# Keys and values as one level of Strassen products in a two-layer decoder trunk

## The chip, the cores and the metric

One core of a Trainium2 chip runs the whole program in one launch. The metric is the device time in microseconds of one execution; lower is better. The median of three timed runs of the kernel before is 1442.52 us (1442.39 to 1442.74).

## The reference

Two layers; `x` is 512 tokens by 1024 features, all in float32. Of each layer this matters here:

```
h = rmsnorm(x) * (1 + sc1(c)) + sh1(c)          # 1024 features
u = h @ w_in                                    # pool, conv, q, k, v (512 columns each of q, k, v), 3 x 1024 gate logits
k = rope(rmsnorm(k)); q = rope(rmsnorm(q))      # 8 heads of 64
y_attn = block-sparse attention(q, k, v)
merged = sig(gate1)*(y_pool @ p_pool) + sig(gate2)*(y_conv @ p_conv) + sig(gate3)*(y_attn @ p_attn)
x = x + g1(c) * (merged @ w_out)                # g1, sc1, sh1, ...: rows of c_act @ w_ada
x = x + g2(c) * SwiGLU(...)
```

## The kernel before, in words

**Products.** Every float32 product is made of three TensorE matmuls at a faster type: each operand is split into a high part (rounded by ScalarE) and a low part (the rest, by VectorE), and `mm3` adds high*high, high*low and low*high. Activations are kept as 8 tiles of 128 features by 512 tokens, `norm.hi[k]` and `norm.lo[k]` (called `big` in the rows). A weight chunk is 128x1024: it is fetched into `raw` by SyncE's DMA queue, its high part `whi` is an ACTIVATE (L328), its low part `wlo` a TENSOR_TENSOR (L331). Chunks of gate columns get their low part by a transfer that adds onto a negated high part instead (`split_by_transfer`, L339 to L343).

**Order on TensorE.** It is written out by hand and kept: q with the first pool and conv columns, four more column tiles, then keys and values, then pool and conv tiles with the attention's pieces between them, the 16 gate tiles of the first two branches, the third gate's 8 tiles (`GATE2`), the 8 `attn` tiles with their merges, the 8 `out` tiles, and the feed-forward part (which already uses Strassen-like sums, class `Sums`).

**Keys and values.** `wide()` makes the keys, then a second `wide()` the values: 4 chunks each, 24 matmuls 128x512 a chunk, into four PSUM banks (one for each 128 tokens). Key banks are copied and squared by ScalarE and their squares summed by VectorE (`qk_evac`, L608 to L611). After the keys `rstds` (L597 to L604) and `scale_k` and `rope` (L989, L626 to L629) run on VectorE beside the values.

**Side work.** `bulk` is a queue of VectorE tasks with costs. Each 2048 columns of matmul are a tick, at which tasks are issued as far as a credit allows that grows by `bulk_rate`; `flush_bulk` issues all of them. Before, the eight dots for `g1` (`gains`, L399: one 128x1024 SCALAR_TENSOR_TENSOR on 512 KB of `w_ada`) lie in it: four beside the keys, four beside the values. `fibers` hold the attention's pieces, which are issued by tick as well; `drain` issues what is left of them.

**End of the attention.** Each `attn` tile is 12 matmuls; its merge is a gating (L1033), an addition (L1067) and a split (high part L572 on ScalarE, low part L573 on VectorE) into `merged[j]`, which all 8 `out` tiles read.

VectorE, ScalarE and each DMA queue work strictly in the order in which the program gives them their instructions; the tables further down show that order.

Of the kernel before, what the change touches and what calls it, by code (L numbers as in the profile page):

```python
# [57 lines left out]
NCOL = 74  # L58

# [20 lines left out]
def hybrid_trunk(ctx, tc, xT, ws, ada, cols, pool_w, qk_w, crow, pos, con, out):  # L80
# [210 lines left out]

    def feed_forward():
# [186 lines left out]
    class Norm:  # L479
        def __init__(self, one=False):  # L480
            self.one = one
            self.low = []
            self.acc = bigt(F32)
            self.last = bigt(F32)
            self.sums = [(bigt(), bigt()) for _ in range(1 if one else 2)]
            self.rstd = bigt(F32)
            self.hi = [bigt() for _ in range(KT)]
            self.lo = [bigt() for _ in range(KT)]

# [43 lines left out]
        def apply(self, l, i, k, lo, hi):  # L533
# [14 lines left out]
            if i == 1:  # L548
                A.activation(self.h[k][:, lo:hi], t[:, lo:hi], AF.Identity, bias=sh)
# [11 lines left out]
        def first_lo(self, k):  # L561
            pin(V.scalar_tensor_tensor(self.lo[k], self.t, mod[0][:, SH1, k:k + 1], f32(self.hi[k]),  # L562
                                       op0=ALU.add, op1=ALU.subtract))

# [42 lines left out]
    def qk_evac(which, qk, ss, t, src):  # L607
        A.activation(qk[t][:, which], src.rearrange("p (h d) -> p h d", d=HD), AF.Copy)  # L608
        sq = tmp()
# [221 lines left out]
    for l in range(L):  # L831
# [47 lines left out]
        def wide():  # L879


            pr = ps_pair()
            groups = [ps_mm(), ps_mm(), pr[:, 0], pr[:, 1]]
            for c in range(4):
                w = next_w()
                order = [(kk, t) for kk in range(2) for t in range(TT)]
                for kk, t in sorted(order, key=lambda o: o[1]) if c == 3 else order:
                    k = 2 * c + kk
                    mm3(groups[t], cut(norm.k(k), slice(None), slice(t * P, (t + 1) * P)),
                        wrow(w, 4 * kk), k == 0, k == KT - 1)  # L890
            return groups
# [79 lines left out]
        gains = ada_tasks(l, (G1,))  # L971
        bulk.extend(gains[:4])
        k_ps = wide()
        for t in range(TT):
            qk_evac(1, qk, ss, t, k_ps[t])
        flush_bulk()
# [14 lines left out]
        bulk.append((1.6, rstds))  # L991
        for t in range(TT):
            bulk.append((1.5, lambda t=t: (scale_k(t), rope(qk, t, wc, wsn))))
        bulk.extend(gains[4:])


        v_ps = wide()
        v = [[bigt().rearrange("p (n h d) -> p n h d", n=4, h=2) for _ in range(TT)] for _ in range(2)]
        for t in range(TT):
            for half in range(2):  # L1000
                src = v_ps[t][:, half * BLOCK:(half + 1) * BLOCK].rearrange("p (n d) -> p n d", d=HD)
                o = v[half][t]
                A.activation(o[:, :, 0], src, AF.Copy)
                V.tensor_sub(o[:, :, 1], src, f32(o)[:, :, 0])
        flush_bulk()


        m01, y_attn = [], []
        fibers.append([3, attention(l, qk, v, nrq, prq, y_attn)])
# [13 lines left out]

        def gate():
            g = ps_mm()
            feature_tile(g, next_w())
            sg = bigt(F32)
            A.activation(sg, g, AF.Tanh, scale=0.5)  # L1028
            return sg
# [21 lines left out]
        sg2 = {}  # L1051
        merged = []
        aw_ = None
        for step, j in GATE2:
            if step == "gate":
                sg2[j] = gate()
                continue
            if j == 0:
                drain()
            if j % 2 == 0:  # L1060
# [74 lines left out]
        n2.h = [bigt(F32) for _ in range(KT)]  # L1135
# [251 lines left out]
```

## Time and profile before

| | before |
|---|---|
| median of runs | 1442.52 us |
| profiled execution, own time | 1442.24 us |
| its span in the trace | 1440.5 us |
| TensorE / VectorE / ScalarE busy | 1433.7 / 1014.5 / 714.0 us |
| instructions on TensorE / VectorE / ScalarE | 8346 / 1858 / 1199 |
| moved by DMA | 241.83 MB, mean 168 GB/s |

The execution's own time is 1.74 us longer than the span between the first and last instruction of the trace. All other times are read from that span's start. A row of the timeline gives start, duration, engine, line, operation, the tile written and the tiles read, and in brackets how long the engine had been idle and what released it.

### The profile page before, as it was taken

What the parts mean: (1) busy time and instruction counts of PE and PEld (TensorE: products, weight loads), DVE (VectorE), ACT (ScalarE), POOL (GpSimd) and SP (SyncE); (2) the same over time, 40 slices, a digit from 0 to 9 for tenths busy, and PEclk for the clock granted to TensorE, in tenths of its full rate; (3) what the DMA queues carried; (4) which work ended last, traced back from release to release, by engine and by line L of the source; (5) the groups of instructions that cost most, each with busy time, mean ns of one, the idle gap of its engine ahead of it and who ended that gap; (6) DMA issues with size and microseconds to landing.
All of it is one profiled execution on the core that took longest, in us unless ns stands there. A gap on an engine that the chain in (4) does not pass through costs nothing.

```text
span 1440.5 us, 21954 instructions
## 1 busy us (share of the span) xinstructions
PE 1433.7 (100%) x8346; PEld 1261.7 (88%) x8346; DVE 1014.5 (70%) x1858; ACT 714.0 (50%) x1199; POOL 145.7 (10%) x204
## 2 busy tenths in 40 slices
PE   9999999999999999999999999999999999999999
PEld 7888888888988998999988888888889989999997
DVE  8887777649686867677798766654578747657663
ACT  5645666733653452535444466666336625525450
POOL 0000110101100311210000000011020102111200
PEclk9999999999999999999999999999999999999999
DMA  9647876665347766756536565567372537637532
GB/s 351 216 149 209 220 184 168 181 229 163 90 140 223 187 179 206 190 146 198 189 125 207 177 146 135 135 154 194 129 208 85 136 114 180 173 105 187 136 88 85
DMA packets 91049, 241.83 MB, mean 168 GB/s; under 512 B 11576, under 2 KB 24256, under 8 KB 90944
## 3 DMA queue, kind: packets, MB, share of 16 engines
q1 hardware_dynamic: 67312, 177.37, 36.8%
q0 software_dynamic: 23040, 62.93, 22.3%
q8 instruction: 65, 1.06, 0.3%
q14 instruction: 40, 0.33, 0.1%
q10 hardware_dynamic: 592, 0.14, 0.0%
HBM read 238.30 MB, written 2.10 MB: 167 GB/s over the span
## 4 chain that ended last, share of the span: by engine, by line
PE 96%; issue 1%; DMA 1%; DVE 1%; ACT 0%; ACTq 0%; DVEq 0%; POOLq 0%
PE mm L151 83%; PE pair L151 12%; PE mm L157 1%; DMA wlo<-in_ws 1%; DMA colt<-in_cols 0%; DVE big L788 0%; DVE big L795 0%; DVE big L562 0%; ACT whi L339 0%; DVE w L399 0%; ACT big L1028 0%; DVE wlo L331 0%; ACT big L575 0%; DVE tmp L555 0%; ACT big L559 0%
## 5 line engine op out<-in xcount | busy, mean ns | idle before, releaser
L151 PE MATMUL mm<-big,whi 128*128 128x512 f32 (+1 forms) x4350 | 1078.0, 339 | 1.0 <-ACT big L1028 1.0
L151 PEld LDWEIGHTS mm<-big,whi 128*128 128x128 f32 x4350 | 744.3, 190 | 87.8 <-issue 2.6
L151 PE MATMUL mm<-big,wlo 128*128 128x512 f32 (+1 forms) x2175 | 735.3, 338 | 0.1
L151 PEld LDWEIGHTS mm<-big,wlo 128*128 128x128 f32 x2175 | 412.6, 190 | 45.3 <-DMA wlo<-in_ws 0.5
L328 ACT ACTIVATE whi<-raw 128x1024 fp32r<-128x1024 f32 (+2 forms) x192 | 198.2, 1034 | 223.2 <-PE mm L151 116.8
L331 DVE TENSOR_TENSOR wlo<-raw,whi 128x1024 fp32r<-128x1024 f32 (+2 forms) x192 | 225.8, 1187 | 53.1 <-ACT whi L328 52.6
L328 ACT ACTIVATE whi<-w 128x1024 fp32r<-128x1024 f32 x72 | 76.2, 1058 | 139.5 <-PE mm L151 85.8
L1073 DVE SCALAR_TENSOR_TENSOR x<-mm,mod,x 128x512 f32<-128x512 f32 (+1 forms) x89 | 61.6, 694 | 75.2 <-PE mm L151 75.0
L399 DVE SCALAR_TENSOR_TENSOR w<-w,csil 128x1024 f32<-128x1024 f32 x80 | 95.9, 1221 | 17.8 <-DMA w<-in_ada 17.7
L331 DVE TENSOR_TENSOR wlo<-w,whi 128x1024 fp32r<-128x1024 f32 x72 | 86.8, 1221 | 28.8 <-ACT whi L328 28.1
L257 POOL DMA_DIRECT2D w<-in_ws x72 | 47.2, 673 | 465.1 <-DVE wlo L331 214.4
L343 POOL DMA_DIRECT2D wlo<-in_ws x48 | 41.0, 855 | 438.1 <-ACT wlo L341 241.5
L259 POOL DMA_DIRECT2D w<-in_ws x72 | 63.4, 906 | 159.0 <-DMA w<-in_ws 155.3
L151 PE MATMUL pair<-whi,big 128*128 128x512 f32 x224 | 76.7, 389 | 0.0
L339 ACT ACTIVATE whi<-raw 128x1024 fp32r<-128x1024 f32 x48 | 51.0, 1063 | 49.4 <-PE mm L151 32.1
L151 PE MATMUL pair<-big,whi 128*128 128x256 f32 (+1 forms) x376 | 74.0, 294 | 0.0
L151 PEld LDWEIGHTS pair<-big,whi 128*128 128x128 f32 x376 | 60.4, 191 | 2.2
L151 PE MATMUL mm<-whi,big 128*128 128x512 f32 x160 | 56.9, 392 | 0.6 <-ACT big L559 0.4
L1033 DVE SCALAR_TENSOR_TENSOR big<-big,mm 128x512 f32<-128x512 f32 x48 | 32.8, 684 | 33.1 <-PE mm L151 31.8
L151 PE MATMUL pair<-big,wlo 128*128 128x256 f32 (+1 forms) x188 | 55.3, 294 | 0.0
L341 ACT ACTIVATE wlo<-whi 128x1024 fp32r<-128x1024 f32 x48 | 50.8, 1059 | 0.3
L151 PEld LDWEIGHTS pair<-whi,big 128*128 128x128 f32 x224 | 42.1, 188 | 8.6
(212 smaller groups left out, 1349.3 us busy)
## 6 DMA issues: line engine op xcount, KB each, us to landing
raw<-in_ws SPq DMA_DIRECT2D x146, 512.0 KB, 4.4
w<-in_ada SPq DMA_DIRECT2D x80, 512.0 KB, 5.5
w<-in_ws POOLq DMA_DIRECT2D x144, 256.0 KB, 4.7
wlo<-in_ws POOLq DMA_DIRECT2D x48, 512.0 KB, 6.8
raw<-in_ws SPq DMA_DIRECT2D x64, 256.0 KB, 4.1
raw<-in_ws SPq DMA_DIRECT2D x24, 384.0 KB, 3.6
raw<-in_ada SPq DMA_DIRECT2D x16, 512.0 KB, 4.4
raw<-in_ws SPq DMA_DIRECT2D x16, 448.0 KB, 5.5
```

The lines of the kernel that those rows point to most:

```text
L151: tc.keep_in_program_order(T.matmul(*a, **k))
L157: tc.keep_in_program_order(T.transpose(*a))
L257: nc.gpsimd.dma_start(dst, self.source(0, 1))
L259: nc.gpsimd.dma_start(dst, self.source(*other), accum_op=ALU.add)
L328: A.activation(hi[:, :n], raw[:, :n], AF.Copy)
L331: ins = V.tensor_sub(lo[:, :n], raw[:, :n], f32(hi)[:, :n])
L339: A.activation(hi[:, :n], raw[:, :n], AF.Copy)
L341: A.activation(lo[:, :n], f32(hi)[:, :n], AF.Copy, scale=-1.0)
L343: nc.gpsimd.dma_start(lo[:, i:i + m].rearrange("p b n -> p (b n)"), src, accum_op=ALU.add)
L399: return V.scalar_tensor_tensor(aw, aw, 1.0, csil, op0=ALU.mult, op1=ALU.mult, accum_out=mod[l][:, part, j:j + 1])
L1033: V.scalar_tensor_tensor(sg, sg, 1.0, branch, op0=ALU.add, op1=ALU.mult)
L1073: V.scalar_tensor_tensor(x[k][:, lo:hi], src, mod[l][:, part, k:k + 1], x[k][:, lo:hi], op0=ALU.mult, op1=ALU.add)
```

## The change

Let the 1024 features, the 512 tokens and the 1024 columns (keys, then values) be halved. Instead of eight products of halves, seven are made ("forms": B21, B11, R1, -V, B22, T3, T4), each of two chunks and 24 matmuls. Four forms read sums of halves of `h` (R1, -V, T3, T4; made by `sums_one` and `sums_two`), and four (R1, -V, B22, T3) sums of quarters of the weights (class `KeyValue`). For the sums `norm.h` keeps `h` unsplit, which adds an ACTIVATE for each tile. The finished blocks are put together by additions. T3 and T4 go into the same PSUM pair, T4 on top of T3 after a copy of T3.

The pool and conv work that lay in `bulk` waits till the values are done; `rstds` and the ropes come after B22. The eight `g1` dots are queued once the attention has drained. Two third-gate tiles come ahead of the pool and conv tiles. All other matmuls stay as they are.

```diff
+    class KeyValue:
+        SUBS = 14
...
+        def summed(self, tile, other, cp):
+            flat = tile.rearrange("p b n -> p (b n)")
+            nc.gpsimd.dma_start(flat, self.source(0, 1, cp))
+            nc.gpsimd.dma_start(flat, self.source(other[0], other[1], cp), accum_op=ALU.add)
...
+        def load(self, sub):
+            form, cp = divmod(sub, 2)
+            if sub == 0:
+                self.x = [w4([P, C_BLOCKS, P]) for _ in range(2)]
+                for i in range(2):
+                    self.summed(self.x[i], (1, 1), i)
...
+            if form in (2, 3):
+                w = split_w(self.x[cp], C_BLOCKS)
+                more = self.near[cp] if form == 2 else self.raw(1, 0, cp)
+                pin(V.tensor_add(self.x[cp], self.x[cp], more))
...
+    def squares(which, ss, t, src):
         sq = tmp()
         A.activation(sq, src, AF.Square)
         V.tensor_reduce(ss[:, t, which, :], ...)
...
-        def wide():
...
+        def sums_one(c):
+            h1, h2 = norm.h[c], norm.h[HK + c]
+            one, two = bigt(F32), bigt(F32)
+            r1, nv, t3 = one[:, :BLOCK], one[:, BLOCK:], two[:, :BLOCK]
+            V.tensor_sub(t3, h2[:, BLOCK:], h1[:, BLOCK:])
+            V.tensor_sub(r1, h1[:, :BLOCK], h1[:, BLOCK:])
+            V.scalar_tensor_tensor(nv, t3, -1.0, h1[:, :BLOCK], op0=ALU.mult, op1=ALU.subtract)
+            return one, two, split_from(one)
+
+        def sums_two(c, one, two):
+            V.scalar_tensor_tensor(two[:, BLOCK:], one[:, BLOCK:], -1.0, norm.h[HK + c][:, :BLOCK],
+                                   op0=ALU.mult, op1=ALU.subtract)
+            return split_from(two)
...
+            for cp in form(e, "B21", True):
+                made[cp] = sums_one(cp)
+            for cp in form(a, "B11", True):
+                made[2 + cp] = sums_one(2 + cp)
+            for t in range(2):
+                A.activation(qk[t][:, 1], heads(a[t]), AF.Copy)
+                V.tensor_add(qk[t][:, 1], qk[t][:, 1], heads(e[t]))
+                squares(1, ss, t, qk[t][:, 1].rearrange("p h d -> p (h d)"))
+            for cp in form(c, "R1", True):
+                two[cp] = sums_two(cp, *made[cp][:2])
+            last = [tmp(), tmp()]
+            for t in range(2):
+                A.activation(last[t], c[t], AF.Copy)
+            for cp in form(a, "-V", False):
+                two[2 + cp] = sums_two(2 + cp, *made[2 + cp][:2])
...
+            for _ in form(c, "B22", False):
+                pass
...
+            for _ in form(a, "T3", False):
+                pass
+            for t in range(2):
+                part = tmp()
+                A.activation(part, a[t], AF.Copy)
+                V.tensor_add(last[t], last[t], part)
+            for cp in form(a, "T4", False):
+                if cp == 0:
+                    yield from enumerate(last, 2)
+            yield from enumerate(a)
...
-        gains = ada_tasks(l, (G1,))
-        bulk.extend(gains[:4])
-        k_ps = wide()
...
+        bulk_rate[0], credit[0] = 0.0, -1.0
+        for t, src in keys_values(qk, ss, turn):
...
             if j == 0:
                 drain()
+                bulk.extend(ada_tasks(l, (G1,)))
+                bulk_rate[0] = 1.0
```

Three places of the order follow. The first is VectorE behind the multiplication that ends the last column tile ahead of the keys. Before (a `mm` tile is a PSUM bank, `L399` a `g1` dot, `L331` the low part of a chunk, `L943` and `L920` the conv and pool chains):

```order
L331 TENSOR_TENSOR wlo_759<-raw_755,whi_757 128x1024
L471 SCALAR_TENSOR_TENSOR rope_672<-rope_669,rope_672 128x32
L943 SCALAR_TENSOR_TENSOR big_773<-big_750,colt,big_773 128x511
L472 TENSOR_SCALAR rope_672<-rope_672 128x32
L915 COPY big_821<-big_777 128x1
L943 SCALAR_TENSOR_TENSOR big_773<-big_750,colt,big_773 128x510
L473 TENSOR_SCALAR rope_672<-rope_672 128x32
L399 SCALAR_TENSOR_TENSOR w_779,mod_116<-w_779,csil 128x1024
L476 COPY cosc<-cosc 128x4x8
L399 SCALAR_TENSOR_TENSOR w_782,mod_116<-w_782,csil 128x1024
```

After, the stretch from the first chunk's low part to the low part of the third sum of `h` (`L394` is now the low part of a chunk, `L339` an addition on a weight sum, `L951` to `L953` the sums of `h`, `L637` the low part of such a sum, `L994` the addition that finishes keys):

```order
L394 TENSOR_TENSOR wlo_820<-w_611,whi_818 128x1024
L339 TENSOR_TENSOR w_610<-w_610,raw_705 128x1024
L339 TENSOR_TENSOR w_611<-w_611,raw_742 128x1024
L637 TENSOR_TENSOR big_841<-big_835,big_840 128x512
L394 TENSOR_TENSOR wlo_846<-w_610,whi_844 128x1024
L951 TENSOR_TENSOR big_867<-big_156,big_152 128x256
L339 TENSOR_TENSOR w_610<-w_610,raw_848 128x1024
L952 TENSOR_TENSOR big_866<-big_152 128x256
L953 SCALAR_TENSOR_TENSOR big_866<-big_867,big_152 128x256
L994 TENSOR_TENSOR w_576<-w_576,pair_788 128x512
L994 TENSOR_TENSOR w_577<-w_577,pair_788 128x512
L637 TENSOR_TENSOR big_872<-big_866,big_871 128x512
```

The dots and the pool and conv chains have gone from the stretch; sums, weight additions and splits have come, and the low part of the fourth sum (`big_903`) is eight rows further on.

The second place is ScalarE at the end of the values in layer 0, after (`L391` and `L402` are high parts of chunks, `L404` the negated high part of a gate chunk, `L677` squares, `L1015` the copies of T3, `L1127` values):

```order
L677 ACTIVATE tmp_1043<-w_578 128x512
L677 ACTIVATE tmp_1047<-w_579 128x512
L404 ACTIVATE wlo_1054<-whi_1052 128x1024
L402 ACTIVATE whi_1091<-raw_1089 128x1024
L404 ACTIVATE wlo_1093<-whi_1091 128x1024
L391 ACTIVATE whi_1122<-raw_1120 128x1024
L1015 ACTIVATE tmp_1114<-pair_789 128x512
L1015 ACTIVATE tmp_1117<-pair_789 128x512
L1127 ACTIVATE big_782<-tmp_958 128x4x64
```

Before, this place of ScalarE's queue held the high parts and the values' copies without a bank that had to be read before it was written again:

```order
L339 ACTIVATE whi_1047<-raw_1045 128x1024
L341 ACTIVATE wlo_1049<-whi_1047 128x1024
L339 ACTIVATE whi_1084<-raw_1082 128x1024
L341 ACTIVATE wlo_1086<-whi_1084 128x1024
L1003 ACTIVATE big_1118<-mm_936 128x4x64
L1003 ACTIVATE big_1122<-mm_936 128x4x64
L1003 ACTIVATE big_1119<-mm_937 128x4x64
L1003 ACTIVATE big_1123<-mm_937 128x4x64
L1003 ACTIVATE big_1120<-pair_935 128x4x64
```

The two L1015 copies are new, stand behind `whi_1122`, and read the pair into which T4's matmuls go on adding.

The third is VectorE at the last merges of layer 0, before (`L1033` gating, `L1067` addition, `L573` low part, `L331` a chunk's low part):

```order
L1067 TENSOR_TENSOR big_3081<-big_3081,big_2247 128x512
L573 TENSOR_TENSOR big_3263<-big_3047,big_3262 128x512
L573 TENSOR_TENSOR big_3282<-big_3081,big_3281 128x512
L331 TENSOR_TENSOR wlo_3289<-raw_3285,whi_3287 128x1024
L1033 SCALAR_TENSOR_TENSOR big_3161<-big_3161,mm_3291 128x512
L1067 TENSOR_TENSOR big_3161<-big_3161,big_2430 128x512
L1033 SCALAR_TENSOR_TENSOR big_3194<-big_3194,mm_3310 128x512
L1067 TENSOR_TENSOR big_3194<-big_3194,big_2612 128x512
L573 TENSOR_TENSOR big_3307<-big_3161,big_3306 128x512
L573 TENSOR_TENSOR big_3326<-big_3194,big_3325 128x512
```

After (`L1161`, `L1197`, `L637` the same three, `L462` a `g1` dot, `L394` a chunk's low part):

```order
L637 TENSOR_TENSOR big_3374<-big_3152,big_3373 128x512
L394 TENSOR_TENSOR wlo_3381<-raw_3377,whi_3379 128x1024
L462 SCALAR_TENSOR_TENSOR w_3390,mod_116<-w_3390,csil 128x1024
L1197 TENSOR_TENSOR big_3239<-big_3239,big_2643 128x512
L1161 SCALAR_TENSOR_TENSOR big_3278<-big_3278,mm_3405 128x512
L637 TENSOR_TENSOR big_3402<-big_3239,big_3401 128x512
L462 SCALAR_TENSOR_TENSOR w_3412,mod_116<-w_3412,csil 128x1024
L1197 TENSOR_TENSOR big_3278<-big_3278,big_2818 128x512
L503 TENSOR_TENSOR mod_116<-mod_116,colt 128x8
L507 TENSOR_SCALAR mod_116<-mod_116 128x8
L394 TENSOR_TENSOR wlo_3468<-raw_3464,whi_3466 128x1024
L637 TENSOR_TENSOR big_3424<-big_3278,big_3423 128x512
```

Dots now stand between the parts of the merges, and a chunk's split has come ahead of the last merge's low part (the last row).

## Rows read from the trace of the kernel before

**Rows 1.** The page, parts 1, 4 and 6 (KB each, us from issue to landing)

```profile
PE 1433.7 (100%) x8346; PEld 1261.7 (88%) x8346; DVE 1014.5 (70%) x1858; ACT 714.0 (50%) x1199; POOL 145.7 (10%) x204
...
PE 96%; issue 1%; DMA 1%; DVE 1%; ACT 0%; ACTq 0%; DVEq 0%; POOLq 0%
...
raw<-in_ws SPq DMA_DIRECT2D x146, 512.0 KB, 4.4
w<-in_ada SPq DMA_DIRECT2D x80, 512.0 KB, 5.5
```

**Rows 2.** What TensorE waited for in the whole span

```profile
PE pair L151 <- POOL ones L203: 1.1, 1, 1.1
PE mm L151 <- ACT big L1028: 1.0, 2, 0.5
```

**Rows 3.** Busy time of each engine in two stretches of layer 0

```profile
core 0: us, PE busy (x) PEld busy (x) DVE busy (x) ACT busy (x) POOL busy (x), PEclk, DMA share, GB/s
72.00:115.00 43.00, 43.00 (x191) 35.62 (x190) 35.95 (x90) 17.78 (x26) 1.84 (x2) 1.00 0.51 168
300.00:335.00 35.00, 35.00 (x156) 29.01 (x155) 20.69 (x29) 11.95 (x16) 0.00 (x0) 1.00 0.43 149
```

**Rows 4.** Timeline of TensorE, start and end of keys and values, layer 0

```profile
71.95 0.39 PE L151 MATMUL mm<-whi,big 128*128 128x512 f32 x1
...
115.47 0.61 PE L151 MATMUL mm<-big,whi 128*128 128x512 f32 x2
```

**Rows 5.** Timeline of VectorE beside keys and values, layer 0

```profile
72.15 0.69 DVE L966 TENSOR_TENSOR big<-mm,big 128x512 f32<-128x512 f32 x1
72.76 0.17 DVE L476 COPY sins<-sins 128x32 f32<-128x32 f32 x1
...
76.40 1.22 DVE L399 SCALAR_TENSOR_TENSOR w<-w,csil 128x1024 f32<-128x1024 f32 x1
...
84.16 2.36 DVE L331 TENSOR_TENSOR wlo<-raw,whi 128x1024 fp32r<-128x1024 f32 x2
...
103.27 0.42 DVE L627 TENSOR_TENSOR tmp<-w,rtab 128x256 f32<-128x256 f32 x1
103.61 0.42 DVE L626 TENSOR_TENSOR tmp<-w,rtab 128x256 f32<-128x256 f32 x1
```

**Rows 6.** Timeline of ScalarE beside keys and values, layer 0

```profile
89.83 0.60 ACT L608 ACTIVATE w<-mm 128x512 f32<-128x512 f32 x1 [0.25 <-PE mm L151]
90.33 0.59 ACT L610 ACTIVATE tmp<-mm 128x512 f32<-128x512 f32 x1
...
111.33 1.06 ACT L341 ACTIVATE wlo<-whi 128x1024 fp32r<-128x1024 f32 x1
112.30 0.36 ACT L1003 ACTIVATE big<-mm 128x256 fp32r<-128x256 f32 x1
```

**Rows 7.** Timeline of VectorE, start of the keys, layer 1

```profile
782.10 0.69 DVE L966 TENSOR_TENSOR big<-mm,big 128x512 f32<-128x512 f32 x1 [3.37 <-PE mm L151]
```

**Rows 8.** Timeline of TensorE, first attn tile and first out tile, layer 0

```profile
301.77 0.61 PE L151 MATMUL mm<-big,whi 128*128 128x512 f32 x2
...
334.41 0.62 PE L151 MATMUL mm<-big,whi 128*128 128x512 f32 x2
```

**Rows 9.** Timeline of VectorE, merges of layer 0

```profile
321.01 0.69 DVE L1033 SCALAR_TENSOR_TENSOR big<-big,mm 128x512 f32<-128x512 f32 x1 [5.94 <-PE mm L151]
...
331.90 1.22 DVE L331 TENSOR_TENSOR wlo<-raw,whi 128x1024 fp32r<-128x1024 f32 x1
...
336.05 1.37 DVE L573 TENSOR_TENSOR big<-big,big 128x512 fp32r<-128x512 f32 x2
337.34 2.35 DVE L331 TENSOR_TENSOR wlo<-raw,whi 128x1024 fp32r<-128x1024 f32 x2
```

**Rows 10.** Timeline of VectorE, first and last merge of layer 1

```profile
1015.83 0.69 DVE L1033 SCALAR_TENSOR_TENSOR big<-big,mm 128x512 f32<-128x512 f32 x1 [6.07 <-PE mm L151]
...
1047.19 1.37 DVE L573 TENSOR_TENSOR big<-big,big 128x512 fp32r<-128x512 f32 x2
```

More of the change, by code (lines that the diff above doesn't have):

```diff
@@ L58 @@
 NCOL = 74
+KEYS = 12
+AHEAD = 2
+SOON = [20 + 2 * KT + j for j in range(AHEAD)]
 SH1, SC1, G1, SH2, SC2, G2 = range(6)
@@ L488, in __init__ @@
             self.lo = [bigt() for _ in range(KT)]
+            self.h = [bigt(F32) for _ in range(KT)]
         def add(self, k, lo, hi):
@@ L608, in qk_evac @@
         A.activation(qk[t][:, which], src.rearrange("p (h d) -> p h d", d=HD), AF.Copy)
+        squares(which, ss, t, src)
+    def squares(which, ss, t, src):
         sq = tmp()
@@ new lines, in sums_two, with keys_values, rows, form @@
+        def sums_two(c, one, two):
+            V.scalar_tensor_tensor(two[:, BLOCK:], one[:, BLOCK:], -1.0, norm.h[HK + c][:, :BLOCK],
+                                   op0=ALU.mult, op1=ALU.subtract)
+            return split_from(two)
+        def keys_values(qk, ss, then):
+            early, late = slice(0, BLOCK), slice(BLOCK, S)
+            made = [None] * HK
+            two = [None] * HK
+            def rows(name, c):
+                if name in ("R1", "-V"):
+                    return cut(made[c][2], slice(None), early if name == "R1" else late)
+                if name in ("T3", "T4"):
+                    return cut(two[c], slice(None), early if name == "T3" else late)
+                return cut(norm.k(c if name == "B11" else HK + c), slice(None),
+                           late if name == "B22" else early)
+            def form(o, name, start):
+                for cp in range(2):
+                    w = next_w()
+                    for t in range(2):
+                        for i in range(2):
+                            c = 2 * cp + i
+                            mm3(o[t], cut(rows(name, c), slice(None), slice(t * P, (t + 1) * P)), wrow(w, 4 * i),
+                                start and c == 0, c == HK - 1, skip_group_check=not start)
+                    yield cp
+            e, a = ps_pair(), ps_pair()
+            e, a, c = [e[:, 0], e[:, 1]], [a[:, 0], a[:, 1]], [ps_mm(), ps_mm()]
+            heads = lambda t: t.rearrange("p (h d) -> p h d", d=HD)
+            for cp in form(e, "B21", True):
[13 more added lines that the diff above has]
+                two[2 + cp] = sums_two(2 + cp, *made[2 + cp][:2])
+            for t in range(2):
+                A.activation(qk[2 + t][:, 1], heads(a[t]), AF.Copy)
+            for _ in form(c, "B22", False):
+                pass
+            for t in range(2):
+                V.tensor_add(qk[2 + t][:, 1], qk[2 + t][:, 1], heads(c[t]))
+                squares(1, ss, 2 + t, qk[2 + t][:, 1].rearrange("p h d -> p (h d)"))
+            then()
+            for _ in form(a, "T3", False):
+                pass
+            for t in range(2):
+                part = tmp()
[5 more added lines that the diff above has]
+            yield from enumerate(a)
@@ L1055, in hybrid_trunk @@
             if step == "gate":
-                sg2[j] = gate()
+                if j not in sg2:
+                    sg2[j] = gate()
                 continue
@@ L1134, in hybrid_trunk @@
         n2 = Norm()
-        n2.h = [bigt(F32) for _ in range(KT)]
         table(AF.Abs_reciprocal_sqrt, t[:, 0:1])
```

94 lines of the change are left out of this document (58 added, 36 removed).

## The prediction

> **What bounds the kernel now.** I read the page first: TensorE is busy 1433.7 of 1440.5 us and makes 96% of the chain that ended last, while VectorE is at 70% and ScalarE at 50% [rows 1]. Then what TensorE waited for: its longest wait is 1.1 us at the very start, the next 1.0 in all [rows 2]. So every matmul that goes is worth its whole pitch, and every wait that comes costs its whole length. Third, the two stretches that the change touches: beside keys and values TensorE is busy 43.00 of 43 us and VectorE 35.95; from the attn tiles on, 35.00 of 35 and 20.69 [rows 3]. The reader is to see that the mean of 70% is no cover in the first stretch: VectorE is at 84% there before anything is added. The timelines [rows 4 to 10] give the durations.
>
> **Matmuls: the saving.** Keys and values of layer 0 run from 71.95 to 115.47 us [rows 4], 43.52 us for 192 matmuls, 0.2267 each, without a gap. After there are 7 forms of 24, 168 in all. 24 x 0.2267 = 5.44 us less in a layer, 10.88 in both. The other matmuls keep their number, and two gate tiles only change places. The chunks grow from 8 of 5.44 us to 14 of 2.72.
>
> **Durations.** An operation begins on VectorE 0.08 before the one ahead ends: a 512-wide one of 0.69 takes 0.61 (72.15 to 72.76), a 1024-wide one 1.14 (two in 2.36), a 256-wide one 0.34 (103.27 to 103.61) [rows 5]. ScalarE: 0.97 for 1024 (111.33 to 112.30), 0.50 for 512 (89.83 to 90.33), and it begins 0.25 after what TensorE releases [rows 6]. The halves of `h` with SCALAR_TENSOR_TENSOR have no row; I take 0.35 (TENSOR_TENSOR 0.34 below, its full 0.42 above). The additions on weights are 1024-wide TENSOR_TENSORs as the split is, 1.14.
>
> **First wait: the sums of R1.** B21 and B11 read `h` itself and run at once, 71.95 to 82.83. R1 needs the four sums of `h`; its second chunk begins at 85.55, and the sixth matmul of it reads the low part of the fourth sum, at 86.69. On VectorE's queue the multiplication at 72.15 waits for the last column tile, and from there to that low part stand, in the order of the program: 8 of 1024 (4 splits, 4 weight additions), 9.12 us; 7 of 512 (the multiplication, four low parts, two additions that finish keys), 4.27; two reductions, 1.22; 13 of 256, 4.5; some ten small rotary ones, 1.5. Sum 20.6, so 92.8, with 0.1 for the last write 92.9. TensorE is held 6.2 us, in pieces, the longest some 4 us before the fourth sum's high part. ScalarE's high parts go alongside; where they don't, it gets later, up to 2 us. I keep 4.0 (a walk a tenth shorter) and 8 as ends and take 6.3. In layer 1 VectorE begins at 782.10 after 3.37 idle [rows 7] (keys 0.20 ahead of it, as in layer 0), without the rotary ones but with one 256-wide one more: 19.5 in operations, and about 1.1 for high parts that come late; the end at 802.8 against 796.6, 6.2 held.
> What was removed from the stretch, dots and pool and conv chains, is already out of this count.
>
> **Second wait: T4 behind the copies of T3.** The other forms find their operands made during the first wait. T3 ends at 71.95 + 6 x 5.44 + 6.3 = 110.9 in layer 0. T4's first matmul adds to the bank pair that the two L1015 copies read, and it waits for the second one. These stand behind a chunk's high part that itself waits for T3's last matmul (its buffer): 0.25 + 0.97 + 2 x 0.50, to 113.2. 2.3 us held; 1 if the high part were ahead, 3 at full durations. In layer 1 more stands there: a leftover dot in VectorE's queue reads a buffer that the split behind the fourth sum frees at 803.9; its load lands 5.5 later [rows 1], at 809.4, dot to 810.6, the next split to 811.7; that frees the buffer of T4's second chunk, landing 4.4 later [rows 1], 816.1; high and low part 818.2; then the two additions of B22, 819.5; squares on ScalarE, 820.1, four 1024-wide ACTIVATEs, 824.0, and the copies, 825.0. T3 ends at 820.7, so 4.3 are held; 2.3 if the dot's load comes early, 6 if late.
>
> **Between.** The last rope ends about 126.7 against the first transposes at about the same time: I count 0, up to 2 for both layers. The extra ACTIVATEs for `norm.h` (0.50 to 0.6, eight a layer) lie in ScalarE's gaps of 2 to 4 us; 0, at worst 1. The eight extra weight DMAs a layer (copy and addition, 512 KB) are queued well ahead, and the mean DMA share is 0.51 beside the keys [rows 3].
>
> **Third wait: the dots behind the attention.** In layer 0 the last merge's low part ended at 337.42 (two in 1.37 from 336.05) [rows 9]; the first `out` tile starts at 334.41, 32.64 behind the first `attn` [rows 8], and reads the last merge with its 22nd to 24th matmul, from 339.17. 1.9 us of slack. From the third merge on (321.01) come four dots (4.6) and one more split ahead of that low part (1.14), 5.7 more; about 1.6 of it falls into VectorE's waits for high parts in that stretch. 337.4 + 4.1 = 341.5 against 339.4: 2.2 held, between 0 (more of it in gaps: VectorE has 14 us idle in 35 [rows 3], 5.94 of them ahead of 321.01 [rows 9]) and 4. In layer 1 all eight dots stand ahead of the third merge, beside idle stretches of 6.07 [rows 10]: 0, at most 2.2.
>
> **Sum.** -10.88 + 6.3 + 6.2 + 2.3 + 4.3 + 2.2 = +10.4. The profiled execution's own time is 1442.24 (0.28 below the median of the runs): 1452.7 us.
>
> **Rivals.**
> *The sums keep pace* (the other side). If VectorE gets from the last column tile to the fourth sum in 14.5 us instead of 20.6 (72.15 to 86.69), R1 is never held; that is the point from which it decides. With operations a third shorter the out stage fits too, and the leftover dot's load leaves early: only T4's 2.3 a layer stay, -10.88 + 4.6 = -6.3, 1436.0; with that hidden as well, 1431.4. For it: TensorE makes 96% of the chain, and VectorE also waits in places that I can't all foresee. Against: no operation in rows 5 is that short, and the order is fixed by the program.
> *Half the wait.* 3.5 at R1 in each layer (small operations and 256-wide halves cheaper than taken), 2.3 at each T4, no wait at `out`: +0.7, 1443.0. Rows 3 speak for the `out` part, rows 5 against the first.
> *The clock falls.* The granted clock is 1.00 in both stretches [rows 3] and TensorE never idles over 1.1 us [rows 2], so no row shows what an idle piece of 4 us does. At its 1.2 GHz level instead of 2.4, each matmul takes 0.453; one form so run costs 24 x 0.227 = 5.44 more. Once a layer: 1452.7 + 10.9 = 1463.6; once in all: 1458.1. The page "TensorE: Matmul & The Clock Gate" of the Trainium skill (section "The HAM clock gate") says that the throttled state is the default and that only activity releases it, so it speaks for this rival; the trace of before, which has no such idling behind the start, neither confirms nor refutes it. By that page's own cold pitch, 426.7 ns for a 512-wide matmul, one such form would cost an estimated 4.8 us.
>
> **Chances and range.** Forecast, 1447 to 1458: 0.62. Sums keep pace: 0.12. Half the wait: 0.13. Clock: 0.13. What differs by under 0.2% (2.9 us) a measurement of this kernel can't tell from no change: faster is below 1439.6, slower above 1445.4. Faster 0.12 from the first rival; within 0.2% 0.12, most of the second; slower 0.76. The low ends of the unknown terms together give -10.9 + 8.0 + 3.3 = +0.4, 1442.6; the high ends -10.9 + 16 + 9 + 6 + 3, 1465, which won't all come. Range 1442 to 1461; outside it lie the first rival and part of the clock.
>
> **What would show it.** In the profile after, TensorE's waits should have a row of 5 to 13 us on the low or high part of the `h` sums (VectorE L637, ScalarE L636) and one of 4 to 8 on ScalarE L1015, and TensorE's matmuls should take about 1423 us. From the start of B21 to the end of T4 I expect 46.7 us in layer 0 (43.5 before) and about 48.6 in layer 1. VectorE should have no idle time over 0.5 us between the last column tile and the fourth sum's low part, and the first `out` tile a wait of about 2 us on VectorE L637. The prediction is wrong if R1's wait is under 3 us (then the count of VectorE's walk is off), if T4 starts right behind T3, or if a granted clock under 1.00 appears.

## The result and the profile after

The changed kernel takes 1461.22 us (median of 4 runs, 1459.23 to 1463.06), the kernel before 1442.54 on the same chip: ratio 1.0128, 95% interval 1.0113 to 1.0143. It is slower by 18.7 us where I forecast 10.2, and its median lies 0.2 above my range. The profiled execution took 1460.55 us.

The page of after, sections 1 and 4 (engines and chain), against [rows 1]:

```profile
PE 1432.1 (98%) x8298; PEld 1255.4 (86%) x8298; DVE 1062.3 (73%) x1938; ACT 750.2 (51%) x1254; POOL 158.2 (11%) x220
...
PE 87%; DVE 7%; ACT 2%; DMA 2%; issue 1%; ACTq 0%; DVEq 0%
```

48 matmuls fewer, as the change says, which is 10.88 us of matmuls, but TensorE is busy only 1.6 us less: those that are left take longer in places. The chain, 96% TensorE before, now runs 7% through VectorE. What TensorE waited for, against [rows 2] (engine, line waited for: us in all, times, longest):

```profile
PE mm L157 <- ACT big L636: 11.7, 5, 3.8
PE pair L157 <- ACT tmp L1015: 4.4, 2, 2.3
PE mm L157 <- DVE big L637: 2.8, 2, 1.9
PE pair L157 <- DVE big L862: 1.7, 3, 1.2
PE pair L157 <- POOL ones L209: 1.1, 1, 1.1
```

L636 and L637 are the high and low part of a split, here those of the sums of `h` for R1 and, in the out stage, of the merges; L1015 are the copies of T3. TensorE's timeline in layer 0, against [rows 4]: first matmul of the keys, the waits, first matmul behind T4:

```profile
72.88 0.39 PE L157 MATMUL pair<-whi,big 128*128 128x512 f32 x1
...
86.96 0.96 PE L157 MATMUL mm<-whi,big 128*128 128x512 f32 x2 [1.91 <-DVE big L637]
...
91.24 0.50 PE L157 MATMUL mm<-whi,big 128*128 128x512 f32 x1 [1.18 <-ACT big L636]
...
96.33 0.80 PE L157 MATMUL mm<-whi,big 128*128 128x512 f32 x1 [3.80 <-ACT big L636]
96.92 0.63 PE L157 MATMUL mm<-wlo,big 128*128 128x512 f32 x1
97.35 1.05 PE L157 MATMUL mm<-whi,big 128*128 128x512 f32 x2
...
119.23 0.50 PE L157 MATMUL pair<-whi,big 128*128 128x512 f32 x1 [2.12 <-ACT tmp L1015]
...
124.80 0.62 PE L157 MATMUL mm<-big,whi 128*128 128x512 f32 x2
```

Behind the longest wait a matmul takes 0.43 (96.92 to 97.35) instead of 0.2267. Windows show why; the number behind the engines is the granted clock as a share of 2.4 GHz (1.00 in [rows 3]; 0.50 is the lower of the two levels, 1.2), layer 0 and then layer 1:

```profile
84.00:88.00 4.00, 2.09 (x8) 1.45 (x7) 4.00 (x6) 2.64 (x4) 0.55 (x1) 0.91 0.21 62
88.00:92.00 4.00, 2.79 (x7) 1.34 (x6) 4.00 (x9) 2.84 (x5) 1.41 (x2) 0.66 0.77 230
92.00:96.00 4.00, 0.49 (x1) 0.19 (x1) 4.00 (x7) 1.53 (x3) 0.00 (x0) 0.77 0.97 249
96.00:100.00 4.00, 3.67 (x9) 2.82 (x10) 4.00 (x6) 1.39 (x3) 0.85 (x1) 0.50 0.81 188
...
812.00:816.00 4.00, 1.40 (x3) 1.09 (x4) 4.00 (x7) 2.10 (x3) 0.85 (x1) 0.50 0.47 78
816.00:820.00 4.00, 4.00 (x15) 3.20 (x14) 3.46 (x6) 2.69 (x5) 0.00 (x0) 0.78 0.97 312
838.00:842.00 4.00, 4.00 (x13) 3.13 (x12) 4.00 (x10) 1.85 (x5) 0.00 (x0) 0.57 1.03 231
```

VectorE (third engine) is at 4.00 of 4 in all of them but one (816 to 820). VectorE's timeline, against [rows 5]: the multiplication behind the last column tile, and the low part of the fourth sum (from the one to the end of the other is VectorE's walk, 76.74 to 97.04):

```profile
76.74 0.68 DVE L1095 TENSOR_TENSOR big<-mm,big 128x512 f32<-128x512 f32 x1
...
96.37 0.67 DVE L637 TENSOR_TENSOR big<-big,big 128x512 fp32r<-128x512 f32 x1
```

The stretch from the first matmul of the keys to the end of T4, both layers, as windows (same columns):

```profile
72.88:124.80 51.92, 42.85 (x169) 33.44 (x168) 46.61 (x102) 30.50 (x45) 4.51 (x6) 0.90 0.55 144
794.47:844.25 49.78, 42.31 (x170) 33.48 (x169) 44.21 (x85) 28.54 (x40) 4.51 (x6) 0.90 0.62 167
```

The balance of the two profiled spans, 1458.8 against 1440.5: the keys start 0.93 later (the first transfer of the columns landed later; in the runs below that start lies between 71.6 and 72.7, so it is no part of the change); layer 0's stretch takes 51.92 for 43.52, +8.40; layer 1's 49.78, also for 43.52, +6.26; the first `out` tile of layer 0 waits 1.67 and 0.85. Sum 18.1 of 18.3. Without waits and at full clock a stretch would take 168 x 0.2267 = 38.08.

### The profile page after: what moved, and what is told of

It reads as the page before. It is cut to its first block, busy times and chain, and to the rows that moved or that the text cites. A ratio compares the mean times of both kernels' runs of the same rounds, so it can differ in the third digit from the quotient of the medians.

```text
span 1458.8 us, 22043 instructions
## 1 busy us (share of the span) xinstructions
PE 1432.1 (98%) x8298; PEld 1255.4 (86%) x8298; DVE 1062.3 (73%) x1938; ACT 750.2 (51%) x1254; POOL 158.2 (11%) x220
## 4 chain that ended last, share of the span: by engine, by line
PE 87%; DVE 7%; ACT 2%; DMA 2%; issue 1%; ACTq 0%; DVEq 0%
PE mm L157 75%; PE pair L157 10%; DMA raw<-in_ws 2%; DVE wlo L394 2%; PE mm L163 2%; DVE w L462 2%; ACT whi L391 1%; DVE big L637 1%; DVE w L339 0%; ACT big L636 0%; DVE tmp L618 0%; DVE big L625 0%; DVE big L1197 0%; DMA colt<-in_cols 0%; ACT whi L402 0%
## 5 line engine op out<-in xcount | busy, mean ns | idle before, releaser
L391 ACT ACTIVATE whi<-raw 128x1024 fp32r<-128x1024 f32 (+2 forms) x192 | 198.3, 1033 | 193.6 <-PE mm L157 110.9
L394 DVE TENSOR_TENSOR wlo<-raw,whi 128x1024 fp32r<-128x1024 f32 (+2 forms) x192 | 226.2, 1186 | 57.7 <-ACT whi L391 57.3
L391 ACT ACTIVATE whi<-w 128x1024 fp32r<-128x1024 f32 x84 | 88.9, 1058 | 160.2 <-PE mm L157 90.9
L394 DVE TENSOR_TENSOR wlo<-w,whi 128x1024 fp32r<-128x1024 f32 x84 | 101.2, 1220 | 28.7 <-ACT whi L391 28.0
L462 DVE SCALAR_TENSOR_TENSOR w<-w,csil 128x1024 f32<-128x1024 f32 x80 | 95.6, 1220 | 14.0 <-DMA w<-in_ada 14.0
L157 PE MATMUL pair<-whi,big 128*128 128x512 f32 x256 | 85.0, 397 | 4.4 <-ACT tmp L1015 4.4
L402 ACT ACTIVATE whi<-raw 128x1024 fp32r<-128x1024 f32 x48 | 50.8, 1058 | 30.5 <-PE mm L157 27.8
L157 PEld LDWEIGHTS pair<-whi,big 128*128 128x128 f32 x256 | 49.0, 192 | 15.6 <-ACT tmp L1015 5.3
L636 ACT ACTIVATE big<-big 128x512 fp32r<-128x512 f32 x52 | 32.3, 625 | 38.4 <-DVE big L1197 22.4
L404 ACT ACTIVATE wlo<-whi 128x1024 fp32r<-128x1024 f32 x48 | 50.8, 1057 | 0.4
L157 PE MATMUL mm<-whi,big 128*128 128x512 f32 x96 | 38.2, 440 | 12.7 <-ACT big L636 10.1
```

What stands on the lines that cost most here:

```text
L157: tc.keep_in_program_order(T.matmul(*a, **k))
L391: A.activation(hi[:, :n], raw[:, :n], AF.Copy)
L394: ins = V.tensor_sub(lo[:, :n], raw[:, :n], f32(hi)[:, :n])
L402: A.activation(hi[:, :n], raw[:, :n], AF.Copy)
L404: A.activation(lo[:, :n], f32(hi)[:, :n], AF.Copy, scale=-1.0)
L462: return V.scalar_tensor_tensor(aw, aw, 1.0, csil, op0=ALU.mult, op1=ALU.mult, accum_out=mod[l][:, part, j:j + 1])
```

## The experiments

Theory: VectorE has more to do beside keys and values than the shorter matmuls leave time for; TensorE idles, and behind the idle pieces the granted clock falls. Rivals: the order is at fault (the sums stand too late in VectorE's queue); late transfers are; the clock alone is. Times are medians; before was 1442.35 to 1442.61 beside them. "Stretch" is as above.

**e2_busy: is it the clock?** Spare matmuls in R1's idle pieces, nothing else:

```diff
+ if name == "R1" and t == 0 and cp == 1:
+     n, g = (6, 15)[i], ps_mm()
+     for m in range(n):
+         matmul(g, norm.hi[0][:, :P], ...
```

> The changed kernel with 21 matmuls 128x512 more in each layer, whose result nobody reads, in the two idle pieces of R1's second chunk (6 ahead of the third sum, 15 ahead of the fourth: 1.36 and 3.40 us of the 9.4 and 6.0 us that R1 is held). Theory (the idle pieces make the granted clock fall to its 1.2 GHz level, which costs 2.3 us net in layer 0 and about 1.8 at R1 of layer 1): the granted clock stays at 1.00 beside R1, and the kernel is 3 to 4 us faster than the changed kernel although it computes more, about 1457.5. Rival (the clock falls for another reason, or its loss is hidden under the hold): no faster; up to 9.5 us slower if the 42 matmuls don't fit into the holds.

1457.23, ratio 1.0099 (1.0085 to 1.0113): 4.0 us faster than the changed kernel with 42 matmuls more. (Its four runs, 1454.03 to 1459.43, reach just into the changed kernel's, and the profiled one is the slowest.) The clock beside R1 stays 1.00 (windows of this run):

```profile
92.00:96.00 4.00, 3.63 (x15) 2.40 (x14) 4.00 (x8) 2.10 (x3) 0.72 (x1) 1.00 0.89 289
96.00:100.00 4.00, 4.00 (x19) 3.27 (x19) 3.81 (x7) 2.93 (x5) 0.14 (x1) 1.00 0.80 130
```

So idling brings the clock down, and its fall at R1 costs some 4 us. It is a consequence: 14.6 us of loss against the kernel before stay.

**e4_hold and e10_hold: why is VectorE 3.7 late in layer 0?** TensorE releases the multiplication at about 73.1, it begins at 76.74. Beside the column tiles, GpSimd's transfers of the summed weights run (274 GB/s in all between 48 and 54, 127 before), and raw weights that landed 3.3 after their issue before (49.79 to 53.06) take 4.8 (50.88 to 55.67). The high part that waits for them, before and after:

```profile
53.06 1.06 ACT L328 ACTIVATE whi<-raw 128x1024 fp32r<-128x1024 f32 x1 [0.22 <-DMA raw<-in_ws]
```

```profile
55.67 1.06 ACT L391 ACTIVATE whi<-raw 128x1024 fp32r<-128x1024 f32 x1 [1.57 <-DMA raw<-in_ws]
```

e4 asks for the transfers one or two chunks later in the program; e10 ties them to the first column tile's multiplication.

```diff
  e4:  -     self.summed(self.x[i], (1, 1), i)      (at sub == 0)
       + if sub in (1, 2):
       +     self.summed(self.x[sub - 1], (1, 1), sub - 1)
  e10: + nc.gpsimd.tensor_copy(flat[:, :1], behind[:, :1])   (ahead of the transfer; behind is
                                                              the first multiplication's tile)
```

> The changed kernel with the two summed weight transfers of 1 MB each (four DMAs of 512 KB on GpSimd's queue, begun at 48 to 55 us in layer 0) put one and two chunks later. Theory (they slow the landing of the column tiles' weights, so that VectorE reaches the multiplication that ends the last column tile at 76.7 us instead of 73.1, which lengthens R1's hold in layer 0 from 6 to 9.4): that multiplication at 73.1 to 74.5, R1's hold 2 to 3.5 us shorter in layer 0, layer 1 as it was: about 1458 to 1459. Rival (the eight extra ACTIVATEs for h make the splits late): no change, 1461. If the summed weights themselves land too late for R1, slower.

> The changed kernel with the four summed-weight transfers of R1 on GpSimd's queue held behind the multiplication of the first column tile (about 61 us instead of 48). If these transfers make the raw weights of the column tiles late, VectorE's multiplication behind the last column tile begins within 0.8 us of TensorE's release instead of 3.7 late, and R1 of layer 0 is held about 6 us instead of 9.4: 1457 to 1458.5. If the added ScalarE work for h makes it late, the lateness and the hold stay: 1460 to 1462. If the transfers now land too late, TensorE or VectorE waits for R1's weights behind 83 us: 1462 or more.

e4: 1459.39, but the transfers were issued at 47.4 to 55.1, hardly otherwise than in the changed kernel (48.3 to 55.2), each when its buffer was free: inconclusive. e10: 1465.12, ratio 1.0159 (1.0145 to 1.0173). VectorE, then ScalarE, in its timeline:

```profile
72.26 0.69 DVE L1099 TENSOR_TENSOR big<-mm,big 128x512 f32<-128x512 f32 x1 [0.41 <-PE mm L157]
```

```profile
76.89 1.06 ACT L395 ACTIVATE whi<-w 128x1024 fp32r<-128x1024 f32 x1 [4.78 <-DMA w<-in_ws]
```

The multiplication now begins when TensorE releases it: the transfers had made it late, not the activations for `h`. But they land too late for the splits, as the expectation's third case had it, and more is lost than won.

**e1_sums_early, e5_copies: the order alone.** e1 makes the sums beside the column tiles and finishes the keys behind -V; e5 queues the copies of T3 ahead of the next high part.

```diff
  e1: - made[cp] = sums_one(cp)   (beside B21, B11)
      + made[c] = sums_one(c)     (beside the column tiles)
  e5: + split_after[0] = A.activation(part, a[t], AF.Copy)
```

> The changed kernel with the sums of h for R1, -V and T3 made while the column tiles ahead of the keys are multiplied, and the two additions that finish the first keys moved behind the splits of R1's weights; no other work is added or left out. Theory (R1 is held by VectorE's queue from the last column tile to the fourth sum, 9.4 us in layer 0 and 6.0 in layer 1): that walk loses about 8 us, R1's hold falls to 0 to 3 us in layer 0 and 0 in layer 1, and with no long idle piece there the granted clock stays at 1.00 beside R1: 1461 - 6.4 to 9.4 - 6.0 - 3 to 4 = about 1443 to 1446. Rival (the loss is the clock's and the transfers' and the sums only happen to be late): R1 starts as late as before behind its weights, and the time stays above 1456.

> The changed kernel with ScalarE's two copies of T3 queued ahead of the next chunk's high part of the weights. If T4 is held because the copies stand behind that high part, its wait falls from 2.1 and 2.3 us to about 1.25 in each layer (0.25 + 2 x 0.50), and the low granted clock beside T4 of layer 1 goes: 1457.5 to 1459.5. If the weights or VectorE set T4's start, the wait only changes its name: 1460 to 1462.

e1: 1468.35, ratio 1.0174, slower than the changed kernel. R1's hold went (3.1 in layer 0, none in layer 1), and waits of 8.2 and 3.2 stood ahead of T4 and one of 5.2 ahead of T3: the weights of T3 and T4 come late instead (ScalarE idles 5.3 us before one in layer 0, 8.2 in layer 1), and ScalarE's copies stand behind them. e5: 1459.78, ratio 1.0116 (1.0103 to 1.0130); T4 waits 1.2 and 1.5 for 2.1 and 2.3, and the clock behind it stays 1.00 in layer 1 (838 to 842). The prediction's reason for that wait holds; it is small, and in time the run can't be told from the changed kernel.

**e11_two_mid: TensorE work between, that VectorE hardly takes part in.** The two third-gate tiles go between B21 and B11 instead of behind T4.

```diff
+ subs[2:2] = [(None, (l, b)) for b in soon[:MID]]      # MID = 2
+ middle()      # feature_tile(held[j], next_w()) for both
  for cp in form(a, "B11", True):
```

> The changed kernel with the two third-gate tiles, 10.9 us of TensorE work that VectorE hardly takes part in, between B21 and B11 instead of behind T4, in both layers. If the loss is that R1 comes before VectorE has the sums, R1's holds of 9.4 and 6.0 us fall under 1.5 in each layer, the clock beside R1 stays 1.00 (4 to 5 us more), T4's waits stay 2.1 and 2.3: 1440 to 1444, no slower than the kernel before. If VectorE or the weights only get later with it, or the attention lacks the two tiles behind T4, waits of 5 us or more stand elsewhere: 1450 or more.

1464.30, ratio 1.0152: each theory was right in one half. Its waits in layer 0, the stretch first, then behind it:

```profile
PE pair L158 <- ACT tmp L1020: 4.8, 1, 4.8
PE mm L158 <- DVE wlo L398: 0.6, 1, 0.6
```

```profile
PE mm L158 <- ACT big L1156: 2.8, 1, 2.8
PE mm L158 <- ACT big L643: 2.6, 1, 2.6
```

R1 waits 0.6 instead of 6.9. Less the tiles' 10.88 us, the stretches take 45.47 and 43.25, 13 us less than in the changed kernel. From layer 0's stretch to layer 1's keys, and from layer 1's stretch to the end, 10.3 and 9.1 us come back. In layer 0 the two waits shown are 5.4 of it, with low clock behind them (0.57 at 148 to 152). That VectorE and ScalarE have work left over, which now meets no gate tiles, is the likely reason; no run tests it.

**e3_before_dots, e6_dots_gates: the out stage.** e3 gives the kernel before only the later dots; e6 spreads them over the gate stage.

```diff
  e3, on before: + bulk.extend(ada_tasks(l, (G1,)))  behind drain()
  e6, on after:  the same line moved to the gate stage, bulk_rate[0] = 0.4
```

> The kernel before with one part of the change alone: the eight g1 dots of each layer behind the attention's drain. Keys and values as before. Theory (the dots stand between the parts of the last merges on VectorE, and the first out tile of layer 0 waits for the last merge's low part): a wait of about 2 to 2.5 us in layer 0 at the first out tile and none in layer 1, so 1442.5 + 2.0 to 2.5 = about 1444.8. Rival (the dots' place costs nothing by itself; the wait in the changed kernel comes from the two gate tiles or from later weights): 1442.5, or a little less, since VectorE is freed beside the keys.

> The changed kernel with the first gate's dots spread over the gate stage of each layer, beside the attention, instead of behind it. If the dots' place among the merges makes the wait at the out stage of layer 0, that wait of 2.5 us goes: 1458 to 1459.5. If VectorE is short beside the attention, new waits of 1 to 3 us stand there: 1460 to 1464.

e3: 1443.10, ratio 1.0003 (0.9994 to 1.0012): no change and no wait there; its last two low parts end at 339.5, against the 339.4 that `out` needs. So the later dots alone cost nothing; the 2.5 us in the changed kernel come from them together with its own order (two merges stand behind dots and splits, the last low part begins at 350.81). e6: 1469.62, slower than both halves of its expectation; the wait in layer 0 went, and in layer 1 TensorE waits 9.3 us beside the attention (4.8 on one VectorE operation).

**e15, e17, e18, e19: VectorE's additions given to transfers.** e15 adds the next weights by GpSimd's accumulating transfers; e17 makes the low parts of B21, B11 and T4 by transfer too; e18 and e19 are e15 and e5 with one gate tile in the middle and two behind T4, or two and none.

```diff
- pin(V.tensor_add(self.x[cp], self.x[cp], more))
+ nc.gpsimd.dma_start(self.x[cp]..., self.source(form - 2, 0, cp), accum_op=ALU.add)
```

> The changed kernel with the eight additions on weights taken off VectorE: GpSimd's accumulating transfers add the next quarter to the summed weights instead. VectorE does four 1024-wide operations (4 x 1.14 = 4.6 us) less between the last column tile and the fourth sum in each layer, and four raw loads a layer go. If R1 is held by VectorE's amount of work, the holds fall from 9.4 and 6.0 us to about 5 and 1.5, with 2 to 4 us of low clock less, against 1 to 3 us of waits for the later weights of -V: 1449 to 1454. If the order or the clock alone makes the loss, or the transfers come too late on ScalarE's queue: 1458 or more.

> As the run before, and the weights of B21, B11 and T4 get their low parts by ScalarE and a transfer, as the gate tiles' do: six more 1024-wide operations (6.9 us) leave VectorE in each layer, and ScalarE has six more (6 x 0.97). If VectorE's amount of work is what bounds the stage, R1 is held under 2 us in each layer and T4 no longer than now: 1444 to 1449. If the work only moves to ScalarE and the queues, waits of the same size stand behind ScalarE's copies: 1454 or more.

> The changed kernel with one third-gate tile between B21 and B11 and two behind T4, the additions on weights by transfer, and ScalarE's copies of T3 ahead of the next high part. One tile is 5.4 us of TensorE work that VectorE has no part in. If the stage is bound by VectorE's amount of work, this is less work and more time: R1 held under 1.5 us, T4 1.3 us, clock 1.00 beside R1: 1440 to 1446. If the waits only move behind T4, as with two tiles there: 1455 or more.

> As the run before, with both third-gate tiles between B21 and B11 and none behind T4. By VectorE's amount of work TensorE has 10.9 us more to do ahead of R1 and 4.6 us less of VectorE to wait for: R1 is not held. What stood behind T4 with the two tiles there (4.8 us at T4, 3 to 4 us each at the next gate and the first conv tile) shrinks to about half with the copies ahead and VectorE 4.6 us sooner: 1446 to 1453. If that wait comes from the missing tiles behind T4 alone, no change against the run with the tiles in the middle: 1460 to 1465.

1459.75, 1474.71, 1457.74 and 1472.91 (ratios 1.0122, 1.0218, 1.0103, 1.0200): three on the rival's side, and e19 slower than either side had it. VectorE is busy only 42.29 us in e15's layer 0, but ScalarE stands before late weights (2.63 and 2.47 idle there) with the sums' high parts queued behind, and R1 waits 5.4. In e17 VectorE is down to 38.22 and 37.80, and the stretches take 58.80 and 53.24. In e18's layer 1, where R1 waits 0.5, the stretch takes 48.06 with one tile of 5.44 in it, 42.6 without: shorter than before, so a shorter stretch is possible in one layer. In layer 0 (57.70) the transfers are late again.

**e21_no_adds, e22_no_low: less work, nothing in its place.** The groups above leave open whether VectorE's amount of work decides.

```diff
  e21: - pin(V.tensor_add(self.x[cp], self.x[cp], more))
  e22: as e21, and  - return split_w(...)   + return high_w(...)   # hi, hi
```

> The changed kernel without the eight additions on weights and with nothing in their place (-V and B22 read the weights of R1): VectorE does 4 x 1.14 = 4.6 us less ahead of the fourth sum in each layer, ScalarE waits for no late weight. If VectorE's amount of work holds R1, the holds fall from 9.4 and 6.0 us to about 5 and 1.5, T4 stays at 2.1 and 2.3, and the clock costs 2 to 4 us less: 1448 to 1453. If VectorE is only late by the order or by other transfers: 1457 or more.

> As the run before, and without the low parts of all fourteen weight chunks of keys and values (the high part is read twice, the matmuls stay as many): VectorE does some 20 us less in each layer's stretch, 8 x 1.14 = 9.1 us less ahead of the fourth sum. If VectorE's amount of work is the cause of R1's holds and so of the clock's falls there, neither is left, T4 waits 2 us or less a layer, and the stretch takes 40 us or less for 38.1 of matmuls: 1436 to 1441, at or under the kernel before. If ScalarE, the transfers or the clock hold it without VectorE: 1448 or more.

1447.67, ratio 1.0037 (1.0024 to 1.0049), and 1441.88, ratio 0.9989 (0.9980 to 0.9998). The stretches of e21, then of e22 (TensorE first, VectorE third, clock behind the engines):

```profile
72.03:118.58 46.55, 41.15 (x169) 32.37 (x168) 41.83 (x98) 29.90 (x44) 3.96 (x5) 0.96 0.60 161
788.14:831.98 43.84, 40.56 (x169) 32.45 (x168) 40.22 (x81) 28.44 (x40) 3.15 (x5) 0.96 0.57 152
```

```profile
72.28:114.38 42.10, 39.98 (x169) 32.61 (x168) 30.53 (x80) 28.32 (x41) 3.08 (x4) 0.96 0.62 166
786.61:827.11 40.50, 38.38 (x170) 31.47 (x169) 28.33 (x70) 28.55 (x40) 2.56 (x3) 1.00 0.58 164
```

Read down VectorE's busy time and the length: 46.61 in 51.92, 44.21 in 49.78, 41.83 in 46.55, 40.22 in 43.84; in these four, where VectorE has more than 38.08 us to do, the stretch is its work plus 3.6 to 5.6. (That is no rule for all runs: where weights come late it is more, 7.7 and 12.2 in e15.) With 30.53 and 28.33 TensorE sets the length, R1 waits for nothing, and T4's 2.1 and its clock are what is left. 4.8 and 4.0 us less on VectorE gave 5.4 and 5.9. VectorE's walk in layer 0 (from the multiplication to the end of the fourth sum's low part), in the changed kernel and in e21:

```profile
76.74:97.04 20.30, 13.35 (x49) 9.50 (x47) 20.27 (x43) 11.32 (x17) 2.58 (x4) 0.84 0.42 123
```

```profile
75.62:90.97 15.35, 12.12 (x50) 8.86 (x48) 15.29 (x39) 9.74 (x15) 2.26 (x3) 1.00 0.56 132
```

VectorE is busy throughout both, and the second is shorter by about the four additions that are gone. R1 is held 4.2 and 1.5 for 9.4 and 6.0 (from where the sixth matmul of its second chunk would begin without a wait to the end of the walk), near the 5 and 1.5 expected.

e22 also says what the change is worth without this work: 0.7 us in the median, since T4 and the out stage (2.4, and the clock behind it) eat the rest of 10.9. Its eleven runs go with their mean granted clock: five at 0.999 or 1.000 take 1438.60 to 1440.54, six at 0.995 to 0.998 take 1441.88 to 1444.67.

**e24_adds_gp, e25_adds_sums_gp: the same work on an engine that is idle.** The chain of additions stays, GpSimd makes them (e25: one operation of each sum too).

```diff
- pin(V.tensor_add(self.x[cp], self.x[cp], more))
+ pin(nc.gpsimd.tensor_add(self.x[cp], self.x[cp], more))
```

> The changed kernel with the eight additions on weights on GpSimd, ahead of its transfers for T3, and ScalarE's copies of T3 ahead of the next high part; everything is computed. VectorE has 4.6 us less to do ahead of the fourth sum in each layer, as in the run that left the additions out (1447.7). If GpSimd takes up to 2.5 us for one and VectorE keeps its durations: 1446 to 1451. If GpSimd takes 4 us or more, or VectorE's operations get longer beside it, -V waits for its weights or R1 stays held: 1455 or more.

> As the run before, and one of the four operations for each sum of h (256 wide, 0.34 us on VectorE) on GpSimd as well. By VectorE's amount of work alone 1.4 us less a layer: 1444 to 1449. If each now adds GpSimd's longer duration to a sum's chain, or waits there behind an addition on weights, the sums come later by 1 to 3 us each: slower than the run before by 2 us or more.

1479.49 and 1477.01, ratios 1.0254 and 1.0234: e24 on the side of its second half, e25 on neither side (2.5 us faster than e24, and far above 1449). GpSimd, then VectorE, in e24's timeline of layer 0:

```profile
80.92 6.83 POOL L339 TENSOR_TENSOR w<-w,raw 128x1024 f32<-128x1024 f32 x2 [18.36 <-DVE wlo L393]
88.92 2.48 POOL L339 TENSOR_TENSOR w<-w,raw 128x1024 f32<-128x1024 f32 x1 [1.17 <-DVE wlo L393]
```

```profile
86.57 2.27 DVE L393 TENSOR_TENSOR wlo<-w,whi 128x1024 fp32r<-128x1024 f32 x1 [3.38 <-ACT whi L390]
...
89.10 2.91 DVE L956 SCALAR_TENSOR_TENSOR big<-big,big 128x256 f32<-128x256 f32 x2
```

A 1024-wide subtraction of 1.22 takes 2.27, two 256-wide operations of 0.42 take 2.91, each beside an addition on GpSimd. So these runs can't tell amount from chain: VectorE lost as much time beside GpSimd as it was spared (46.59 busy in e24's stretch of layer 0, 46.61 in the changed kernel).

## Why the prediction was right and wrong

**Right.** Slower was forecast with 0.76, for the reason that the runs show: VectorE's mean of 70% is no cover beside keys and values. The saving of 24 x 0.2267 a layer is there. The walk from the multiplication to the fourth sum's low part was counted as 20.6 us and took 20.3 (76.74 to 97.04), without a gap; in layer 1 20.7 and 20.6. T4's wait in layer 0 (2.3) measured 2.12, the out stage (2.2) 2.5, layer 1's R1 (6.2) 6.0, counted from the sixth matmul to the last sum.

**Wrong: the clock left out of the sum.** This is the largest miss. The step that failed is in the sum: it counts an idle piece at its own length and the matmuls behind it at full clock. I gave "The clock falls" 0.13 as a rival, though my own sum had idle pieces of 4 us in it. A granted clock under 1.00, the last of the prediction's own signs of being wrong, appeared: it fell in both layers beside R1 and in layer 1 beside T4. The matmuls took up to 0.43 (the rival had 0.453), and TensorE is busy 1432.1 us where 1423 was forecast. Of these 9 us, 3 to 4 lie inside R1's holds and cost nothing; in layer 0 some 2.3 us stand behind the last sum, in layer 1 about 3.3. e2 gives 4.0 for R1's. The cold pitch that the Trainium skill gives in "TensorE: Matmul & The Clock Gate" ("The HAM clock gate"), 426.7 ns, agrees with the 0.43 here; no row of before could show it.

**Wrong: R1 of layer 0, 6.3 held.** It was 9.4 (87.6 to 97.0). The walk's length was right, its start 3.7 late. The step that failed is "The eight extra weight DMAs a layer [...] are queued well ahead", costed at nothing: the four for R1's weights run beside the column tiles, and e10 shows that without them there the multiplication begins on time.

**Mis-sized: T4 of layer 1,** 4.3 forecast, 2.32 measured. The chain through the leftover dot came as counted. VectorE (the fourth sum's low part, the dot), then ScalarE (the copies), then TensorE (T4):

```profile
814.64 0.68 DVE L637 TENSOR_TENSOR big<-big,big 128x512 fp32r<-128x512 f32 x1
...
821.93 1.23 DVE L462 SCALAR_TENSOR_TENSOR w<-w,csil 128x1024 f32<-128x1024 f32 x1 [2.46 <-DMA w<-in_ada]
```

```profile
835.93 1.06 ACT L1015 ACTIVATE tmp<-pair 128x512 f32<-128x512 f32 x2
```

```profile
837.04 0.50 PE L157 MATMUL pair<-whi,big 128*128 128x512 f32 x1 [2.32 <-ACT tmp L1015]
```

Counted from the end of the fourth sum (815.3), the dot begins 6.6 later (forecast 6.6) and the copies end 21.7 later (22.2). But T3 ends 19.4 later instead of 17.9, since R1's last matmuls ran at the low clock: 1.5 of the 2.0 missing here is the clock's time again.

Together: 5.2 more than the 46.7 forecast for layer 0's stretch, 1.2 more than 48.6 in layer 1, 0.3 in the out stage, 0.9 at the start: 7.6 of the 7.9 between 1452.7 and the profiled 1460.55. That slower came out was no luck, since R1's walk was counted right. But the range was 19 us wide; the sum itself was 8.5 short of the median.

**The third wait's reason was half right:** later dots alone (e3) cost nothing, and without them (e6) the wait goes. Its sum sets the reading of the last merge at 339.17 and then counts from 339.4; by 339.17 it would have been 2.3.

**What stays open.** e21 and e22 show that taking work off VectorE gives the loss back, but they also shorten the chain of weight additions, and no run takes the same work off VectorE and keeps that chain. For R1 of layer 0 this doubt falls away, since VectorE has no gap in its walk in which it could have waited for that chain (20.27 busy of 20.30); in layer 1 it is busy 19.61 of 20.58. Behind R1 the doubt stays. No version here that computes everything beats the kernel before; the nearest are the run with spare matmuls, 1457.23, and e18, 1457.74 (their runs overlap).

## What to carry to other kernels

Compare the helper engine's whole work in a stretch with the matmul time that will be left there, not its mean share before: once VectorE has more to do than TensorE, a new order mostly moves the wait; here e1, e11 and e19 each brought a new late operand. Where a sum contains idle pieces of TensorE of some us, put the lower clock behind them into the sum. And a transfer that is issued early is not free: ask what lands beside it.

## What was not expected of the hardware

Work given to GpSimd stopped VectorE: an operation of 0.42 took about 2.5 beside an addition of 2.4 to 2.5 us (2.56 from 94.01 on in e24, beside the addition that begins at 93.88). The Trainium skill ("SBUF — State Buffer", "Who interferes with whom") says that a VectorE instruction with two inputs in SBUF contends with a GpSimd instruction that reads SBUF, over ports that are an exclusive lock. The durations here agree with that: the later one seems to wait for the whole of the other.

Idle pieces of TensorE of 1.9 to 3.8 us brought granted clocks of 0.50 to 0.78 behind them; one of 2.12 ahead of T4 did so in layer 0 of e2 (0.64 at 116 to 120) and in layer 1 of e21 (0.57 at 825 to 829), and not in layer 0 of the changed kernel's profile (a matmul in 0.23 from 119.56 on) or of e21 (1.00 at 112 to 120). So the same piece costs 0 to some 2 us from one execution or layer to the next.
